# A planned 15-product kernel: one product of the first triple among the first plain products, two multiplications set aside, and loads in another order

## The chip, the core and the metric

The kernel runs on one core of one Trainium2 chip. The metric is the device time of one execution in microseconds (us). The core has a matrix engine (PE), a vector engine (DVE), a scalar engine (ACT), GpSimd (POOL) and a sync engine (SP) that only issues transfers and waits. Each engine works through its own instructions in order.

## The reference

```python
batch, m, k, n = 16, 512, 1024, 768
y1 = np.matmul(x, w1)          # x: (16, 512, 1024), w1, w2: (1024, 768)
y2 = np.matmul(x, w2)
return (np.tanh(y1) * y2).astype(np.float32)
```

All inputs and the output are 32-bit floats in HBM.

## The kernel before

**The work.** The 8192 rows of x are 64 row tiles of 128 rows. The columns of both weights are cut into three blocks of 512: `a` (w1's first 512 columns), `b` (w2's first 512) and `g` (the last 256 of w1 beside the last 256 of w2). K is cut into two halves of 512, four slices of 128 each. Everything is multiplied in 16-bit floats and summed in 32-bit PSUM banks, of which there are eight.

**Two ways of multiplying.** The first four row tiles (HEAD = 4) are done plainly: eight matmuls for each tile and block (`plain`, `mm`, L420), tanh on ACT, the multiplication by y2 on DVE. The `b` block of tile 3 is kept for the end. The other 60 row tiles are done three at a time, as 20 triples. For a triple a 3x2 by 2x3 block product would take 18 block products; a table `C_OPS` (L24) does it in 15, `p0` to `p14`, each of four matmuls (`product`, L442), on sums and differences of x blocks (`A_SUMS`, made on DVE by `x_sum`, L411) and of weight blocks (`B_SUMS`, `w_sum`, L402). Between the products ACT copies banks (`c_copy`, L447: names copy..., seed...) and DVE adds them (`c_add`, L450: add...); ACT then takes tanh (t, th) and DVE multiplies (m on 512 columns, mh on 256; `c_mul`, L460). Blocks are named by bits: x block 1, 2 are the two K halves of a triple's row 0, 4 and 8 those of row 1, 16 and 32 those of row 2; weight blocks 1, 2, 4 are a, b, g of the first K half, 8, 16, 32 those of the second. So p7 = x block 16 times weight block 1: the first half of row tile HEAD + 2 = 6 with the first four `a` slices. Its bank is copied by ACT (copy376) into the arena.

**How x and the weights arrive.** The first four x tiles come as half tiles of 32-bit floats on SP's queue (`load_first`, L337), DVE casts each half (`cast_x`), PE transposes it (`transpose_pe`, L368), and ACT or DVE moves the transposed half out of PSUM (`evacuate`, L374). The `a` slices come on ACT's and SP's queues, the `g` slices on SP's, into 14 slots of the `arena`, and are cast by DVE or ACT (`cast_w`). Behind a gate on POOL (L483), which waits for the first `g` cast, POOL's queue loads the eight `b` slices with a cast on the way, then the row tiles 6, 4, 5 whole, also with a cast (`load_x`, L352). Those three are transposed on PE; from row tile 7 on POOL loads and SP transposes by DMA (`transpose`, L377). The load of a later tile waits on POOL for a one-column copy from an earlier transposed tile (`hold_loads`, L480).

**What sets the order.** `Planner` (L75) lists every operation with costs, due times and dependencies, plays them once through, and writes the instructions in the order of the planned starts. The products' order is fixed by hand: `PE_ORDER` for one triple (a plus shifts a product into the next triple's time), `FIRST_ORDER` for the first triple, `LAST_ORDER` for the last; `plan.strict` keeps it. `START`, `lands`, `LANDING` and `hold` are assumed times by which the plan is made; on the chip semaphores decide.

```python
position["p" + entry.rstrip("+"), i] = (i + (entry[-1] == "+")) * 15 + n
...
rows_in = (HEAD + 2, HEAD, HEAD + 1)
...
in_order = on_sp[4:] + late + [f"x{mt}" for mt in rows_in]
```

Output tiles: four for the plain row tiles, nine that the triples take in turn (`out_tile`, L414). SP stores them.

Of the kernel before, what the change touches and what calls it, by code (L numbers as in the profile page):

```python
# [69 lines left out]
FIRST_ORDER = "7 10 1 6 12 9 11 14 8"  # L70
# [156 lines left out]
def kernel(  # L227
# [53 lines left out]
    S_NAMES = [o[3] for o in C_OPS if o[1] in ("copy", "add") and o[3][0] == "s"]  # L281
    arena = once.tile([P, len(S_NAMES) * C_BUFS * F], f32, name="arena")
# [3 lines left out]
    early_x = once.tile([P, len(A_SUMS) * S_BUFS * KH * P // 2], f32, name="early_x")  # L286
    x_first = [early_x[:, mt * K:(mt + 1) * K] for mt in range(HEAD)]
# [8 lines left out]
    def xh_place(mt):  # L296
        return (mt - HEAD) % XH_BUFS

    def xh_before(mt):
        return next((m for m in range(mt - 1, 1, -1) if xh_place(m) == xh_place(mt)), None)  # L300
# [35 lines left out]

    def load_first(e, mt, h):  # L337
        pin(nc.sync.dma_start(x_first[mt][:, half(h)], xf[mt][:, half(h)]))

    def cast_x(e, mt, h):  # L340
        copy(e, xh(mt)[:, half(h)], x_first[mt][:, half(h)])
# [10 lines left out]
    def load_x(e, mt):  # L352
        pin(nc.gpsimd.dma_start(xh(mt), xf[mt]))  # L353
# [87 lines left out]

    def product(e, i, dst, a, b, begins):  # L442
        for k in range(KH):
            pin(nc.tensor.matmul(place(i, dst), x_operand(i, a)[:, k, :], w_rhs(b, k),  # L444
                                 start=begins and k == 0, stop=k == KH - 1, skip_group_check=True))
# [17 lines left out]

    def flag_1(e):
# [18 lines left out]
    def gate(e, s, k):  # L483
        pin(nc.gpsimd.tensor_copy(held, w_cols(s, k)[:, :1]))
# [5 lines left out]
    START = 28.6  # L490
    ORIGIN = START - 6 * SLOT

# [10 lines left out]
    plan.strict = [f"{p}.{i}" for _, i, p in sequence]  # L503
# [7 lines left out]
    in_order = on_sp[4:] + late + [f"x{mt}" for mt in rows_in]  # L511
# [3 lines left out]
    for n in in_order:  # L515
        now += 1.25 if n in in_order[-3:] else size[n[0]]
# [4 lines left out]
    for n, what in enumerate(on_sp):  # L521
# [3 lines left out]
        else:  # L525
            s, k = what[0], int(what[1])
            j = slices.index((s, k))
            old = [slices[i - SLOTS] for i in range(j, j + 1 + (s == "g")) if i >= SLOTS]
            op(f"L{what}", {"sp": 0.05}, 0.1 * n - 100, [], load_w, s, k, int(what[2]) if s == "g" else None, issued=before,
               behind=[f"c{a}{b}" for a, b in old], lands=lands[what])  # L530
    op("gate", {"pool": 0.1}, 0.0, ["c%s%d" % GATE], gate, *GATE)
    for n, what in enumerate(late):
        op(f"c{what}", {"pool": 0.58}, 0.1 * n, [], load_w, "b", int(what[1]), issued=[f"c{late[n - 1]}" if n else "gate"], lands=lands[what])
    for n, mt in enumerate(rows_in):
        op(f"L{mt}", {"pool": 0.58}, 1 + 0.1 * n, [], load_x, mt, issued=[f"L{rows_in[n - 1]}" if n else f"c{late[-1]}"],
           behind=[f"cx{m}{h}" for m in range(2, HEAD) for h in range(2) if xh_place(m) == xh_place(mt)], lands=lands[f"x{mt}"])
# [7 lines left out]
    all_casts = [f"c{s}{k}" for s, k in slices if s != "b"]  # L544
# [19 lines left out]
    for mt in rows_in:  # L564
        for h in range(2):
            by_pe(mt, h, lands[f"x{mt}"] - 2, f"L{mt}")
# [17 lines left out]
    def reuse_out(mt):  # L584
        return [f"st{mt - O_BUFS}"] if mt >= HEAD + O_BUFS else []
# [283 lines left out]
```

## Time and profile before

| | |
|---|---|
| median of 3 runs | 297.97 us (297.73 to 298.39) |
| the profiled execution | 297.88 us, of which the profile's span is 296.3 |
| granted TensorE clock, mean | 0.997 |
| busiest groups of PE | L444, bank<-b,early_x: 640 matmuls, 148.3 us; L444, bank<-b,xT: 240, 58.3 us |
| DMA queue 1 (hardware): 44.84 MB; queue 0 (software) | 16.78 MB |
| x tiles on POOL's queue, issue to landing | 6.8 us median |
| transposes on SP's queue, issue to landing | 6.9 us median |

In a timeline row stand the start in us, the duration, the engine, the line and operation, output<-input, how many instructions were merged, and in brackets the idle time of that engine ahead of the row and what ended it. Matmuls of 512 columns are shown with 0.38 us each though they start closer together, so a merged row hides small gaps. In a row of busy time by stage, each engine has its busy time and, in brackets, its number of instructions; then follow the granted clock, the busy share of the DMA queues (over 1 where several hold an engine) and GB/s. L numbers are lines of the kernel before.

### The profile page before, as it was taken

Reading aid. Unit: us, or ns where it says so; the run is one execution under the profiler, and the core shown is the slowest. Engines: PE = TensorE matmul, PEld = TensorE weight load, DVE = VectorE, ACT = ScalarE, POOL = GpSimd, SP = SyncE. Lnnn points to the kernel's source line nnn. Section 1 sums busy time; section 2 is a strip of 40 time slices with the busy share of each in tenths; the row PEclk is TensorE's granted clock in tenths of the full one; section 3 lists DMA queues with packets and bytes.
Section 4 is the critical chain, followed back from the end, with each engine's and each line's share of the span. In section 5 each row is a group of like instructions: output and inputs, shape, how many; then the busy total and the mean of one; then the engine's idle time right before and its main releaser. Section 6 shows DMA issues by size and latency. Waiting matters only on the chain. (4 is left out here: it accounts for less than half of the span.)

```text
span 296.3 us, 4677 instructions
## 1 busy us (share of the span) xinstructions
PE 289.6 (98%) x1374; PEld 131.9 (45%) x1374; DVE 257.4 (87%) x552; ACT 226.3 (76%) x453; POOL 49.2 (17%) x129
## 2 busy tenths in 40 slices
PE   7999999999999999999999999999999999999994
PEld 3344444444444444444444444444444444444442
DVE  1679899989999998888989898898989989898785
ACT  3586899699978979797797988768686776868442
POOL 0063033020213021102110120031012110000000
PEclk9999999999999999999999999999999999999998
DMA  6999999999999999999999999999999999340334
GB/s 215 388 307 204 183 160 149 229 197 237 224 253 271 215 198 252 237 144 253 233 234 162 221 191 218 195 310 223 221 235 232 261 269 298 127 162 25 136 141 164
DMA packets 84715, 63.51 MB, mean 214 GB/s; under 512 B 62800, under 2 KB 66896, under 8 KB 84688
## 3 DMA queue, kind: packets, MB, share of 16 engines
q1 hardware_dynamic: 73888, 44.84, 62.9%
q0 software_dynamic: 9792, 16.78, 37.2%
q10 hardware_dynamic: 1008, 1.57, 1.5%
q8 instruction: 11, 0.18, 0.3%
q14 instruction: 16, 0.13, 0.2%
HBM read 39.85 MB, written 25.17 MB: 219 GB/s over the span
## 5 line engine op out<-in xcount | busy, mean ns | idle before, releaser
L444 PE MATMUL bank<-b,early_x 128*128 128x512 f16 x640 | 148.3, 379 | 0.1
L444 PEld LDWEIGHTS <-early_x 128*128 128x128 f16 x800 | 78.1, 98 | 95.0 <-issue 0.7
L454 DVE TENSOR_TENSOR bank<-bank,arena 128x512 f32<-128x512 f32 x100 | 69.6, 697 | 14.4 <-ACT arena L448 8.8
L448 ACT ACTIVATE arena<-bank 128x512 f32<-128x512 f32 x100 | 59.4, 596 | 28.7 <-PE bank L444 28.5
L462 DVE TENSOR_TENSOR o<-o,bank 128x256 f32<-128x256 f32 (+1 forms) x132 | 64.3, 512 | 6.1 <-ACT o L457 5.4
L381 ACT ACTIVATE junk<-xh 128x1024 f16<-128x1024 f16 x60 | 63.3, 1054 | 0.2
L444 PEld LDWEIGHTS <-xT 128*128 128x128 f16 x400 | 39.0, 98 | 46.6 <-issue 0.3
L444 PE MATMUL bank<-b,xT 128*128 128x512 f16 x240 | 58.3, 379 | 0.0
L457 ACT ACTIVATE o<-bank 128x256 f32<-128x256 f32 (+1 forms) x80 | 34.5, 436 | 16.0 <-DVE bank L454 11.7
L444 PE MATMUL bank<-wh,xT 128*128 128x512 f16 x160 | 41.1, 379 | 0.0
L444 PE MATMUL bank<-wh,early_x 128*128 128x512 f16 x160 | 40.9, 379 | 0.0
L481 POOL CAST held<-xT 128x1 f32<-128x1 f16 x54 | 12.3, 227 | 159.4 <-DMA xT<-xh 159.3
L353 POOL DMA_DIRECT2D xh<-in_x_dram x60 | 31.9, 532 | 17.2 <-issue 7.7
L412 DVE TENSOR_TENSOR early_x<-early_x,xT 128x512 f16<-128x512 f16 x80 | 33.2, 419 | 0.5
L448 ACT ACTIVATE bank<-bank 128x512 f32<-128x512 f32 x40 | 21.5, 574 | 7.3 <-DVE bank L454 6.2
L457 ACT ACTIVATE o<-arena 128x512 f32<-128x512 f32 x40 | 25.1, 628 | 1.2 <-DVE arena L454 1.2
L421 PE MATMUL bank<-wh,xT 128*128 128x512 f16 x72 | 18.5, 379 | 0.5 <-DVE wh L359 0.3
L412 DVE TENSOR_TENSOR early_x<-xT,xT 128x512 f16<-128x512 f16 x40 | 16.8, 419 | 0.0
L412 DVE TENSOR_TENSOR early_x<-xT,early_x 128x512 f16<-128x512 f16 x40 | 16.8, 419 | 0.0
L454 DVE TENSOR_TENSOR bank<-arena,bank 128x512 f32<-128x512 f32 x20 | 13.9, 695 | 2.4 <-ACT o L457 0.9
L454 DVE TENSOR_TENSOR arena<-bank,arena 128x512 f32<-128x512 f32 x20 | 13.7, 683 | 0.2
L454 DVE TENSOR_TENSOR arena<-arena,bank 128x512 f32<-128x512 f32 x20 | 13.6, 681 | 0.0
(47 smaller groups left out, 134.7 us busy)
## 6 DMA issues: line engine op xcount, KB each, us to landing
out_dram<-o SPq DMA_DIRECT2D x58, 384.0 KB, 5.3
xh<-in_x_dram POOLq DMA_DIRECT2D x60, 256.0 KB, 6.8
arena<-in_w_dram SPq DMA_DIRECT2D x12, 256.0 KB, 5.6
early_x<-in_x_dram SPq DMA_DIRECT2D x8, 256.0 KB, 5.0
arena<-in_w_dram ACTq DMA_DIRECT2D x4, 256.0 KB, 5.9
wh<-in_w_dram POOLq DMA_DIRECT2D x8, 128.0 KB, 5.1
out_dram<-o SPq DMA_DIRECT2D x4, 256.0 KB, 6.5
xT<-xh SPq DMA_TRANSPOSE x57, 6.9
```

Source lines behind the costliest of these rows:

```text
L353: pin(nc.gpsimd.dma_start(xh(mt), xf[mt]))
L381: pin(nc.scalar.activation(junk[:, :src.shape[-1]], src, ACT.Abs, scale=scale, accum_out=sums[:, column:column + 1]))
L412: pin(engine[e].tensor_tensor(x_operand(i, v), x_operand(i, a), x_operand(i, b), OP[how]))
L421: pin(nc.tensor.matmul(bank(chain)[:, :rhs.shape[-1]], xt(mt)[:, k, :], rhs, start=first, stop=k == KO - 1, skip_group_check=True))
L444: pin(nc.tensor.matmul(place(i, dst), x_operand(i, a)[:, k, :], w_rhs(b, k), start=begins and k == 0, stop=k == KH - 1, skip_group_check=T ...
L448: pin(nc.scalar.activation(place(i, dst), place(i, src), ACT.Copy, scale=float(sign)))
L454: pin(nc.vector.tensor_tensor(place(i, dst), a, b, ALU.add if signs == (1, 1) else ALU.subtract))
L457: pin(nc.scalar.activation(out_tile(HEAD + 3 * i + r)[:, lo:lo + n], place(i, src)[:, :n], ACT.Tanh, scale=float(sign)))
L462: pin(nc.vector.tensor_tensor(o, o, place(i, src)[:, at:at + n], ALU.mult))
L481: pin(nc.gpsimd.tensor_copy(held, xt(mt)[:, 0, :1]))
```

## The change

Six things change; the rest follows from them in the plan.

1. The first half of row tile 6 (`x60`) is loaded on SP as 32-bit floats, sixth in order, into a free arena slot (`STAGED`), cast by DVE (`cx60`), transposed by PE and evicted.
2. `p7` of the first triple leaves `FIRST_ORDER` and the strict order; it is due at 13.0, among the plain `a` products. What remains of the first triple is ordered 10 6 1 12 9 11 14 8.
3. POOL's queue carries, behind the gate, `b0 b4 b1 b5 x61 x4 b2 x51 x50 b6 b3 b7`: second half of tile 6, tile 4, the halves of tile 5, with the `b` slices between.
4. `m0` and `m2` of the first triple: ACT copies the bank into an output tile that is still free (those of row tiles 11 and 10), and DVE multiplies from there later.
5. In every triple the row tiles are loaded and transposed in the order 2, 0, 1 instead of 0, 1, 2.
6. A write to an arena slot waits for the casts out of that slot alone, not for all casts; the slots are dealt in another order. Row tile 0 is stored in one piece. The absolute sums of the second triple are due later.

```diff
-FIRST_ORDER = "7 10 1 6 12 9 11 14 8"
+FIRST_ORDER = "10 6 1 12 9 11 14 8"
...
-    LANDING = {HEAD + 6: 5.8, HEAD + 7: 4.1, HEAD + 8: 3.9}
+    LANDING = {HEAD + 6: 4.4, HEAD + 7: 4.1, HEAD + 8: 3.9}
+    rows = list(range(HEAD)) + [HEAD + 3 * i + r for i in range(TRIPLES) for r in (2, 0, 1)]
+    turn = {mt: n for n, mt in enumerate(rows)}
...
+    ASIDE = {"m0": (HEAD + 7, 55.0), "m2": (HEAD + 6, 54.0)}
...
+    S_NAMES.insert(1, S_NAMES.pop(0))
...
+    STAGED = SLOTS - 2
...
     def xh_place(mt):
-        return (mt - HEAD) % XH_BUFS
+        return (turn[mt] - HEAD) % XH_BUFS
...
+    def x_staged(mt, h):
+        return x_first[mt][:, half(h)] if mt < HEAD else arena[:, STAGED * F:(STAGED + 1) * F]
...
-    def load_x(e, mt):
-        pin(nc.gpsimd.dma_start(xh(mt), xf[mt]))
+    def load_x(e, mt, cols=slice(0, K)):
+        pin(nc.gpsimd.dma_start(xh(mt)[:, cols], xf[mt][:, cols]))
...
+    def slot_casts(name):
+        n = S_NAMES.index(name) * C_BUFS
+        return [f"c{s}{k}" for j, (s, k) in enumerate(slices) if s != "b" and n <= j % SLOTS < n + C_BUFS] + [f"cx{HEAD + 2}0"] * (n <= STAGED < n + C_BUFS)
...
+    def c_aside(e, r, src, borrowed):
+        pin(nc.scalar.copy(out_tile(borrowed)[:, :F], place(0, src)))
+
+    def aside_mul(e, r, borrowed):
+        o = out_tile(HEAD + r)[:, :F]
+        pin(nc.vector.tensor_tensor(o, o, out_tile(borrowed)[:, :F], ALU.mult))
...
+    P7 = 13.0
...
+    position["p7", 0] = 0
...
-    plan.strict = [f"{p}.{i}" for _, i, p in sequence]
+    plan.strict = [f"{p}.{i}" for _, i, p in sequence if (p, i) != ("p7", 0)]
+    slot_of[0, "p7"] = P7
...
-    on_sp = "x00 x10 x20 x30 x01 x11 a4 a5 x21 a6 x31 a7".split() + [f"g{k}{t}" for k in range(KH) for t in range(2)]
-    late = [f"b{k}" for s, k in slices if s == "b"]
-    rows_in = (HEAD + 2, HEAD, HEAD + 1)
-    GATE = ("g", 0)
+    on_sp = "x00 x10 x20 x30 x01 x60 x11 a4 a5 x21 a6 x31 a7".split() + [f"g{k}{t}" for k in range(KH) for t in range(2)]
+    by_pool = "b0 b4 b1 b5 x61 x4 b2 x51 x50 b6 b3 b7".split()
+    GATES = {"b0": ("cg0", w_cols("g", 0)[:, :1])}
...
+    op(f"cx{HEAD + 2}0", {"dve": 0.37}, lands["x60"] - 1, ["Lx60"], cast_x, HEAD + 2, 0,
+       behind=[f"cx{m}{h}" for m in range(2, HEAD) for h in range(2) if xh_place(m) == xh_place(HEAD + 2)])
...
-                    before = [f"{r}.{i - C_BUFS}" for r in readers[o[3]]] if i >= C_BUFS else all_casts
+                    before = [f"{r}.{i - C_BUFS}" for r in readers[o[3]]] if i >= C_BUFS else slot_casts(o[3])
...
+            elif i == 0 and name in ASIDE:
+                borrowed, at = ASIDE[name]
+                op(f"y{name}.0", {"act": 0.5}, due + 1, [n for n in needs if n[0] != "t"], c_aside, r, o[4], borrowed, chains=chains)
+                op(f"{name}.0", {"dve": 0.6}, at + 6, [f"y{name}.0"] + [n for n in needs if n[0] == "t"], aside_mul, r, borrowed, hold=at)
+                outs[mt].insert(0, f"{name}.0")
...
-            for t in range(2 if mt < 2 else 0):
+            for t in range(2 if mt == 1 else 0):
...
-    for mt in range(BY_PE, MT):
-        back = xh_before(mt)
+    for n, mt in list(enumerate(rows))[BY_PE:]:
+        back, last, held_by = xh_before(mt), rows[n - 1], rows[max(n - AHEAD, BY_PE)]
```

More of the change, by code (lines that the diff above doesn't have):

```diff
@@ L296, in xh_place @@
     def xh_place(mt):
-        return (mt - HEAD) % XH_BUFS
+        return (turn[mt] - HEAD) % XH_BUFS
     def xh_before(mt):
-        return next((m for m in range(mt - 1, 1, -1) if xh_place(m) == xh_place(mt)), None)
+        return next((m for m in rows[turn[mt] - 1:1:-1] if xh_place(m) == xh_place(mt)), None)
     pin = tc.keep_in_program_order
@@ L514 @@
     now = 9.2
-    for n in in_order:
-        now += 1.25 if n in in_order[-3:] else size[n[0]]
+    for n in arrivals:
+        now += 1.25 if n in by_pool and n[0] == "x" and len(n) == 2 else size[n[0]]
         lands[n] = now + (LAG if now > LAG_FROM else 0.0)
@@ L563 @@
         op(f"D{mt}", {"act": 1.05}, START + 8, [f"Lx{mt}0", f"Lx{mt}1"], abs_x, mt, hold=11 + 4 * mt)
-    for mt in rows_in:
+    for mt in rows[HEAD:BY_PE]:
         for h in range(2):
-            by_pe(mt, h, lands[f"x{mt}"] - 2, f"L{mt}")
+            by_pe(mt, h, x_loads[mt, h][1] - 2 - 0.1 * h * (mt == HEAD + 1), x_loads[mt, h][0])
     def made(mt):
```

61 lines of the change are left out of this document (38 added, 23 removed).

## The prediction

> **What bounds the kernel now.** I read the page's busy shares and the two rows of slices first, then busy time by stage, then the timeline of the first 45 us.
>
> ```profile
> span 296.3 us, 4677 instructions
> ...
> PE 289.6 (98%) x1374; PEld 131.9 (45%) x1374; DVE 257.4 (87%) x552; ACT 226.3 (76%) x453; POOL 49.2 (17%) x129
> ...
> PE   7999999999999999999999999999999999999994
> ...
> DMA  6999999999999999999999999999999999340334
> ```
>
> PE is busy in every slice but the first and the last, so the time is PE's work plus the holes in its queue. A busy share hides small holes, because a matmul's modelled 0.38 us overlaps the next one. So I count matmuls in stages:
>
> ```profile
> core 0: us, PE busy (x) PEld busy (x) DVE busy (x) ACT busy (x) POOL busy (x), PEclk, DMA share, GB/s
> ...
> 48.00:76.00 28.00, 28.00 (x132) 12.60 (x131) 26.55 (x63) 24.72 (x52) 6.82 (x18) 1.00 1.13 208
> 10.63:17.15 6.52, 6.13 (x39) 2.85 (x39) 3.43 (x9) 4.55 (x9) 0.00 (x0) 1.00 1.07 368
> 28.60:37.00 8.40, 8.27 (x56) 4.28 (x55) 7.53 (x18) 6.71 (x14) 0.48 (x2) 1.00 1.12 185
> 37.00:282.00 245.00, 245.00 (x1138) 111.02 (x1136) 222.72 (x476) 197.47 (x399) 40.09 (x107) 1.00 1.05 211
> ```
>
> From 37 to 282 us, 1138 matmuls take 245.00 us: 0.2153 us a slot, 0.861 us a product of four, and no hole. Nothing is to be won there; it can only be lost. The holes lie ahead of 37 us. The granted clock is 1.00 throughout. In the stage of the a products (10.63 to 17.15) the loads set the pace:
>
> ```profile
> 10.73 0.43 DVE L359 CAST xh<-early_x 128x512 f16<-128x512 f32 x1 [0.18 <-DMA early_x<-in_x_dram]
> ...
> 11.50 0.39 PE L371 MATMUL bank<-ident_h,xh 128*128 128x128 f16 x4
> ...
> 11.92 0.59 ACT L357 COPY xT<-bank 128x512 f16<-128x512 f16 x1 [0.28 <-PE bank L371]
> ...
> 12.37 1.03 PE L421 MATMUL bank<-wh,xT 128*128 128x512 f16 x4
> ...
> 13.04 0.43 DVE L359 CAST xh<-early_x 128x512 f16<-128x512 f32 x1 [0.53 <-DMA early_x<-in_x_dram]
> ...
> 13.52 0.40 PE L371 MATMUL bank<-ident_h,xh 128*128 128x128 f16 x4
> ...
> 13.71 0.43 DVE L359 CAST wh<-arena 128x512 f16<-128x512 f32 x1 [0.24 <-DMA arena<-in_w_dram]
> ...
> 14.19 1.02 PE L421 MATMUL bank<-wh,xT 128*128 128x512 f16 x4 [0.27 <-DVE wh L359]
> ...
> 15.05 0.39 PE L371 MATMUL bank<-ident_h,xh 128*128 128x128 f16 x4
> 15.10 0.43 DVE L359 CAST wh<-arena 128x512 f16<-128x512 f32 x1 [0.28 <-DMA arena<-in_w_dram]
> ...
> 15.27 1.11 PE L421 MATMUL bank<-wh,xT 128*128 128x512 f16 x4
> ...
> 16.67 0.43 DVE L359 CAST wh<-arena 128x512 f16<-128x512 f32 x1 [1.15 <-DMA arena<-in_w_dram]
> ...
> 17.15 1.24 PE L421 MATMUL bank<-wh,xT 128*128 128x512 f16 x5
> ```
>
> Each cast on DVE waits for a DMA, and PE for the cast. Four transposes take 0.22 us (15.05 to 15.27). The stage's 39 instructions are 16 transposes (0.88 us), one matmul begun before it, and 22 matmuls (4.74 us): 5.62 us of work in 6.52, so **0.90 us is lost**. The first g product starts at 17.15, 0.05 us behind the cast of 16.67: there too the load ends the wait.
>
> **The change, part by part.** *p7 and its half tile.* The load of row tile 6's first half becomes the sixth on SP, the place whose cast now starts at 10.73. All later loads on SP fall one place back; between 10.73 and 15.10 six places take 4.37 us, 0.73 each, and 13.04 to 13.71 is 0.67. I take **0.70 us** (bounds 0.67 and 0.73). The cast of g0 moves to 17.37 and the first g product to 17.85. Into that stage come p7's four matmuls (0.861) and the half tile's transposes (0.22), 1.08 us that leave the later queue. Since both ends are set by the same load, the gain is 1.08 - 0.70 = **0.38 us**; the loss left in the stage is 0.52.
>
> Does p7 arrive in time? As built, PE runs the transposes at 11.50, then four matmuls and another half tile's transposes, then p7 at 11.50 + 0.22 + 0.22 + 0.86 = 12.80. Its operand is cast by 11.16, evicted by ACT from 11.92 (0.42 behind the transposes, as in the row above) to 12.51: 0.29 us of cover. Behind that eviction ACT holds the next eviction, an absolute sum, p7's copy and another eviction; I cost that at nothing (bounds 0 to 0.3, the cover), because one of the later evictions is handed to DVE, which stood idle 1.15 us before 16.67. The staging slot in the arena is free at 11.16, five microseconds before the first g cast: nothing.
>
> *The loads on POOL.* The gate still hangs on g0's cast, so the stream starts 0.70 us later. In place of eight b slices and then three row tiles it carries b0 b4 b1 b5, half of tile 6, tile 4, b2, the two halves of tile 5, b6 b3 b7.
>
> ```profile
> L350 POOL DMA_DIRECT2D wh<-in_w_dram x8: 537/568/669, 17.5 to 21.3; - x8
> ...
> DMA to landing us min/median/max: 3.9/5.1/5.5
> ...
> L353 POOL DMA_DIRECT2D xh<-in_x_dram x2: 565/580/596, 21.9 to 22.4; - x2
> ...
> DMA to landing us min/median/max: 6.2/6.6/6.9
> ...
> L353 POOL DMA_DIRECT2D xh<-in_x_dram x1: 535/535/535, 24.0 to 24.0; - x1
> ...
> DMA to landing us min/median/max: 6.6/6.6/6.6
> ```
>
> The last b lands at 21.3 + 5.5 = 26.8, the row tiles at 28.1, 29.3 and 24.0 + 6.6 = 30.6: 1.25 us a tile, 0.63 a half or a b. Counting these as units, b7 was the 8th and is now the 13th: one unit before 30.6, and 0.70 later, 30.7. PE reaches its first use, by the built order, after 53 matmuls, 5 half-tile transposes and p10: 17.85 + 11.41 + 1.10 + 0.86 = 31.22. Cover **0.5 us**. Tile 4 ends unit 7: 26.2 + 0.7 = 26.9, used after 43 matmuls and one set of transposes at 27.33: cover **0.4 us**. So I cost the new order at nothing; without cover it costs what the landing slips beyond 0.4.
>
> Halving loads could cost something by itself. The 128 KB b slices land 0.77 us apart (21.4 to 26.8 in seven steps), the 256 KB tiles 1.25: a fixed part of at most 0.3 a load by these rows, 0.6 for the two loads that the stream has more, of which the cover takes 0.5. The Trainium skill puts it higher: "DMA: Bandwidth & Descriptors", section "Anatomy of one DMA — SWDGE (gpsimd) path", fits about 2.0 us fixed per DMA, and its section Bandwidth advises batching to 1 MiB; by that, as an estimate, the two loads would cost 4 us and the sum would be a loss. The steps of 0.77 us disagree with it as long as many loads are in flight.
>
> *The first triple.* Here the other hole lies:
>
> ```profile
> 32.15 1.29 DVE L412 TENSOR_TENSOR early_x<-early_x,xT 128x512 f16<-128x512 f16 x3
> 32.34 4.92 PE L444 MATMUL bank<-b,early_x 128*128 128x512 f16 x20
> ...
> 34.63 0.69 DVE L454 TENSOR_TENSOR bank<-bank,arena 128x512 f32<-128x512 f32 x1
> ```
>
> Twenty matmuls without a hole are 0.38 + 19 x 0.2153 = 4.47 us; the row says 4.92: **0.45 us lost**. p6, second of them, waits for the third of the three sums, which ends at 33.44, against 32.34 + 0.86 = 33.20; p9 waits for the addition that ends at 35.32. In the built order p6 comes behind b7's first use, at 31.44, and its last operand is transposed at 17.85 + 47 matmuls + four sets of transposes + p10 = 29.71, evicted by 30.72 and summed by 31.25 if DVE is free. DVE is 90% busy there, so I leave 0.15 us and take **0.30** (bounds 0 and 0.45). p9 now has p1, p12 and two plain matmuls between it and p6: its addition has two microseconds.
>
> *Two multiplications set aside.*
>
> ```profile
> L435 DVE TENSOR_TENSOR o<-o,y 128x512 f32<-128x512 f32 x3 | 2.1, 685 | 0.0
> L431 ACT COPY y<-bank 128x512 f32<-128x512 f32 x3 | 1.6, 624 | 0.0
> ...
> 42.30 0.74 DVE L462 TENSOR_TENSOR o<-o,bank 128x256 f32<-128x256 f32 x2
> ```
>
> DVE is spared two pairs of 0.74 us near 43 us and given two of 0.69 near 58; ACT gets two copies of 0.62. PE has no hole in either place, so this is worth nothing by itself (0 to 0.3 lost, if ACT's copies push back an eviction). The stores of tiles 4 and 6 go out later, and no one waits: nothing. The end of the program keeps its order but for eight narrow matmuls moved up among products: nothing, plus or minus 0.1.
>
> The sum on the profiled execution of 297.88: 297.88 - 0.38 - 0.30 = 297.20. The median shown, 297.97, is 0.09 above that execution, so **297.3**.
>
> **The rivals.** *The later loads take it back.* If the POOL stream slips by about 0.9 us more than I reckon, PE waits 0.5 at tile 4 or b7 and little is left: about 297.8. For it: the cover is only 0.4 to 0.5, and DMA share is over 1.0 in each stage above. Against: the bytes are the same, and the stream kept close to 0.63 us a unit through slices and tiles alike.
>
> *Rows in the order 2, 0, 1 (slower).* p7 wants row 2 first, but DVE's sums want rows 0 and 1, and these now come one transposition later. In the fifth triple:
>
> ```profile
> L378 SPq DMA_TRANSPOSE xT<-xh x1: 1471/1471/1471, 60.9 to 60.9; - x1
> ...
> DMA to landing us min/median/max: 7.5/7.5/7.5
> ...
> L378 SPq DMA_TRANSPOSE xT<-xh x1: 1982/1982/1982, 65.5 to 65.5; - x1
> ...
> DMA to landing us min/median/max: 8.5/8.5/8.5
> ...
> 73.64 0.42 DVE L412 TENSOR_TENSOR early_x<-early_x,xT 128x512 f16<-128x512 f16 x1
> ```
>
> The sum at 73.64 reads row 1, which landed at 68.4 and would land third, at 74.0. DVE, ahead by 0.7 us now, would stand about 1.0 us, with the additions for p13 and the evictions that free banks behind it. The third and the fourth triple stand about as close, and three such waits, 3 us, meet 28.00 - 26.55 = 1.45 us of DVE slack from 48 to 76, and some 1.6 us reach PE: 297.3 + 1.6 = **298.9**. It decides once the waits pass that slack. Against: the first PE product that needs such a sum comes microseconds later, and p7's own row comes earlier.
>
> *p7 is not early in effect.* If its eviction comes over 0.3 us late, PE, which runs in order, waits in front of it, and the 0.38 is gone: 297.6 to 297.7.
>
> *A fixed price per load.* If each load paid by itself what the first b paid from issue to landing, 3.9 us, the two more would put b7 7.8 us late, 7.3 beyond its cover: 304.6. The steps of 0.77 us speak against it. By the skill's 2.0 us it would be 300.8.
>
> **How the numbers follow.** Forecast 0.62 (by itself 297.0 to 297.7: the bounds of 0.38, of 0.30 and of the end, not all losses at once); loads take it back 0.15; row order 0.13; p7 late 0.08; fixed price 0.02. The range 296.8 to 298.3 holds the forecast, the first and the third rival, and the mildest outcomes of the second. About 0.2%, 0.60 us, is what can be told from no change. Below 297.37 lies some 0.45, most of the forecast's mass; beyond 298.57 the row order and the fixed price, 0.13 rounded down for the row order's milder outcomes; between, 0.42.
>
> **What would show it.** The g0 cast at 17.3 to 17.4 and the first g product at 17.8 to 17.9, with p7 among the a products and 0.5 us lost in that stage. PE without a hole from there to 31 us. The run of first products short of its 0.45 loss. Still 0.2153 us a slot from 37 us on. I am wrong if PE waits for a DMA between 24 and 32 us, if DVE's sums wait for a transposition between 48 and 76 and the slots there widen, or if the first g product comes later than 18.2.

## The result, and the profile after

The changed kernel takes 302.88 us in the median of 22 runs (297.89 to 321.91), the kernel before 297.86 us beside it (297.64 to 304.70, 22 runs). The ratio is 1.0063, 95% interval 1.0045 to 1.0081: **slower by 0.6%, about 1.9 us**, where 0.7 us less had been forecast. By the medians of all runs it is 5.0 us. The ratio leaves out every run more than 1.5% above the fastest of its kernel, 12 of the 22 after (the profiled execution of 305.15 us below among them) and one of the 22 before, so a hole in this profile counts only where a variant's profile of a run that stays shows the same. In the rows of a run, L numbers are lines of that run's own kernel: in the changed one L456 is a product, L420 a sum of x blocks, L469 tanh, L466 an addition, L474 a multiplication.

The page of the changed kernel: the span, PE's busy time, and the slices of PE and of the transfers.

```profile
span 303.6 us, 4689 instructions
...
PE 292.0 (96%) x1374; PEld 132.3 (44%) x1374; DVE 255.4 (84%) x552; ACT 224.5 (74%) x454; POOL 50.8 (17%) x130
...
PE   7999999999999999998979999999999999999992
...
DMA  6999999999999999999999999999999999941234
```

The same 1374 matmuls stand in 7.3 us more. Busy time by stage says where, first after, then before (columns as in the prediction):

```profile
10.63:17.58 6.95, 6.95 (x47) 3.69 (x46) 4.29 (x11) 6.08 (x12) 0.00 (x1) 1.00 1.07 371
28.60:37.00 8.40, 8.40 (x47) 3.94 (x45) 8.01 (x18) 5.04 (x11) 1.26 (x3) 1.00 1.05 188
...
62.00:92.00 30.00, 29.55 (x136) 12.99 (x135) 27.28 (x66) 25.50 (x56) 5.25 (x13) 1.00 1.18 206
92.00:136.00 44.00, 44.00 (x205) 19.97 (x204) 39.97 (x84) 36.66 (x77) 7.28 (x19) 1.00 1.19 190
136.00:160.00 24.00, 20.45 (x86) 8.66 (x85) 15.69 (x35) 15.19 (x32) 4.11 (x11) 0.93 1.13 212
```

```profile
62.00:92.00 30.00, 30.00 (x141) 13.62 (x140) 28.15 (x66) 26.89 (x58) 5.01 (x15) 1.00 1.16 220
92.00:136.00 44.00, 44.00 (x206) 19.92 (x205) 40.25 (x83) 36.77 (x75) 8.90 (x24) 1.00 1.17 224
136.00:160.00 24.00, 24.00 (x113) 10.92 (x112) 21.42 (x46) 20.36 (x42) 3.59 (x11) 1.00 1.22 228
```

From 62 to 92 us PE starts 136 matmuls instead of 141: 5 x 0.2153 = 1.1 us lost. From 136 to 160 it loses 27 more, 5.8 us, which belongs to this execution. The rest is at the two ends. The start, by the timeline of the changed kernel, then one row of the kernel before:

```profile
10.70 0.43 DVE L367 CAST xh<-arena 128x512 f16<-128x512 f32 x1 [0.25 <-DMA arena<-in_x_dram]
...
12.83 1.03 PE L456 MATMUL bank<-wh,xT 128*128 128x512 f16 x4
...
17.08 0.43 DVE L367 CAST wh<-arena 128x512 f16<-128x512 f32 x1 [0.74 <-DMA arena<-in_w_dram]
17.58 1.24 PE L429 MATMUL bank<-wh,xT 128*128 128x512 f16 x5
...
37.82 1.03 PE L456 MATMUL bank<-wh,xT 128*128 128x512 f16 x4
```

```profile
38.85 1.03 PE L444 MATMUL bank<-wh,xT 128*128 128x512 f16 x4
```

p7 of the first triple runs at 12.83, the first g cast at 17.08, and p7 of the second triple at 37.82 instead of 38.85: **the start gains 1.03 us**, more than forecast. Then the transpositions. SP's transposes of the third and of the fifth triple, after; below, the third triple's before:

```profile
L386 SPq DMA_TRANSPOSE xT<-xh x3: 1270/1950/2817, 40.6 to 45.4; - x3
...
DMA to landing us min/median/max: 4.2/6.3/7.4
...
L386 SPq DMA_TRANSPOSE xT<-xh x3: 1232/1302/2558, 58.1 to 66.1; - x3
...
DMA to landing us min/median/max: 3.3/8.7/10.4
```

```profile
L378 SPq DMA_TRANSPOSE xT<-xh x3: 1344/2178/2521, 41.0 to 45.7; - x3
...
DMA to landing us min/median/max: 4.1/5.9/7.1
```

The last of the third triple lands at 45.4 + 4.2 = 49.6, and before at 45.7 + 4.1 = 49.8. **PE comes 1.0 us earlier, the rows come 0.2 us earlier.** In the fifth triple the third transposition lands at 66.1 + 8.7 = 74.8. What waits for it, what stands around it, and what happens later in this execution:

```profile
58.78 1.29 DVE L481 TENSOR_TENSOR o<-o,o 128x512 f32<-128x512 f32 x2
...
71.95 0.63 ACT L469 ACTIVATE o<-arena 128x512 f32<-128x512 f32 x1 [0.88 <-DMA out_dram<-o]
...
73.12 1.02 PE L456 MATMUL bank<-wh,early_x 128*128 128x512 f16 x4 [0.25 <-ACT bank L460]
...
74.91 0.43 DVE L420 TENSOR_TENSOR early_x<-early_x,xT 128x512 f16<-128x512 f16 x1 [1.51 <-DMA xT<-xh]
...
77.76 0.59 PE L456 MATMUL bank<-wh,xT 128*128 128x512 f16 x2 [0.16 <-ACT o L469]
...
138.11 1.15 ACT L469 ACTIVATE o<-arena 128x512 f32<-128x512 f32 x2 [2.57 <-DMA out_dram<-o]
...
153.08 0.63 ACT L469 ACTIVATE o<-arena 128x512 f32<-128x512 f32 x1 [4.08 <-DMA out_dram<-o]
...
154.25 1.08 PE L456 MATMUL bank<-b,early_x 128*128 128x512 f16 x4 [2.11 <-ACT arena L460]
```

DVE's sum of row 1 waits 1.51 us, and ACT's tanh waits four times for the store of an output tile: 0.88 us at 71.95, 2.57 at 138.11, 4.08 at 153.08, just ahead of PE's longest stop, and 1.0 at 168. From 40 to 92 us PE's loss is four holes: 0.16 us at 41.4, 0.20 at 64.1, 0.41 at 73.1 (behind the store), 0.33 at 77.8 (behind the late row). No wait for a transfer stands ahead of the one at 64.1: DVE had been busy without a break of 0.1 us since 54.6, the 1.29 us of the two set-aside multiplications included. In the kernel before, DVE has time to spare at that place:

```profile
61.47 0.70 DVE L454 TENSOR_TENSOR bank<-bank,arena 128x512 f32<-128x512 f32 x1 [0.26 <-PE bank L444]
62.78 0.75 DVE L462 TENSOR_TENSOR o<-o,bank 128x256 f32<-128x256 f32 x2 [0.61 <-ACT o L457]
```

Last, the end. The changed kernel's transfers from 298 us on and its last stores, then the same of the kernel before:

```profile
GB/s 307 73 22 22 29 51 307 395 410 322 359 329 329 461 329 322 329 322 293 139 7 7 15 7 22 22 22 22 29 15 0 0 0 0 0 0 0 0 0 0
...
q8 instruction: 1, 0.02, 1.0%
...
L426 SPq DMA_DIRECT2D out_dram<-o x2: 332/332/332, 298.3 to 299.0; - x2
...
DMA to landing us min/median/max: 2.3/3.7/3.7
```

```profile
q8 instruction: 1, 0.02, 1.2%
...
L418 SPq DMA_DIRECT2D out_dram<-o x2: 332/332/333, 292.4 to 293.1; - x2
...
DMA to landing us min/median/max: 2.0/2.1/2.2
```

The last stores take 3.7 us instead of 2.2. Each slice of the GB/s row is 0.14 us: the bulk moves at some 330 GB/s until 300.7, and then 10 slices, 1.4 us, at 7 to 29, about a sixteenth, as of one of sixteen engines that is behind. Queue q8 (its kind is "instruction") carries program code, 16 KB a time, 11 times in either kernel. Its last fetch starts at 299.9 us in the changed kernel, among these stores; in the kernel before at 288.6 (the second q8 row is of 285 to 289.4 us), ahead of them. From the issue of the last store to the end of the span it is 303.6 - 298.96 = 4.6 us, before 296.3 - 293.10 = 3.2: **1.4 us lost at the very end**.

### The profile page after: what moved, and what is told of

Read it like the earlier page. It is cut to its first block, busy times and chain, and to the rows that moved or that the text cites. A ratio compares the mean times of both kernels' runs of the same rounds, so it can differ in the third digit from the quotient of the medians.

```text
span 303.6 us, 4689 instructions
## 1 busy us (share of the span) xinstructions
PE 292.0 (96%) x1374; PEld 132.3 (44%) x1374; DVE 255.4 (84%) x552; ACT 224.5 (74%) x454; POOL 50.8 (17%) x130
## 5 line engine op out<-in xcount | busy, mean ns | idle before, releaser
L456 PE MATMUL bank<-b,early_x 128*128 128x512 f16 x640 | 148.5, 379 | 2.1 <-ACT arena L460 2.1
L456 PEld LDWEIGHTS <-early_x 128*128 128x128 f16 x800 | 78.3, 98 | 99.0 <-issue 5.4
L466 DVE TENSOR_TENSOR bank<-bank,arena 128x512 f32<-128x512 f32 x100 | 69.6, 696 | 19.2 <-ACT arena L460 16.3
L474 DVE TENSOR_TENSOR o<-o,bank 128x256 f32<-128x256 f32 (+1 forms) x128 | 61.9, 516 | 9.2 <-ACT o L469 7.1
L460 ACT ACTIVATE arena<-bank 128x512 f32<-128x512 f32 x100 | 57.8, 597 | 15.4 <-PE bank L456 15.3
L456 PEld LDWEIGHTS <-xT 128*128 128x128 f16 x400 | 39.1, 98 | 48.7 <-issue 3.8
L456 PE MATMUL bank<-b,xT 128*128 128x512 f16 x240 | 59.1, 383 | 0.0
L469 ACT ACTIVATE o<-bank 128x256 f32<-128x256 f32 (+1 forms) x80 | 34.8, 440 | 24.1 <-DVE bank L466 22.2
L456 PE MATMUL bank<-wh,early_x 128*128 128x512 f16 x160 | 41.8, 385 | 1.7 <-ACT bank L460 1.7
L456 PE MATMUL bank<-wh,xT 128*128 128x512 f16 x160 | 41.0, 379 | 0.2 <-ACT o L469 0.2
L500 POOL CAST held<-xT 128x1 f32<-128x1 f16 x54 | 13.4, 247 | 162.5 <-DMA xT<-xh 162.4
L469 ACT ACTIVATE o<-arena 128x512 f32<-128x512 f32 x40 | 25.1, 631 | 16.9 <-DMA out_dram<-o 8.5
L361 POOL DMA_DIRECT2D xh<-in_x_dram x61 | 32.7, 537 | 19.4 <-issue 5.5
L420 DVE TENSOR_TENSOR early_x<-early_x,xT 128x512 f16<-128x512 f16 x80 | 33.6, 421 | 2.0 <-DMA xT<-xh 1.5
L429 PE MATMUL bank<-wh,xT 128*128 128x512 f16 x72 | 19.5, 379 | 0.3 <-ACT xT L365 0.2
L420 DVE TENSOR_TENSOR early_x<-xT,xT 128x512 f16<-128x512 f16 x40 | 16.8, 420 | 0.0
L420 DVE TENSOR_TENSOR early_x<-xT,early_x 128x512 f16<-128x512 f16 x40 | 16.8, 419 | 0.0
L466 DVE TENSOR_TENSOR arena<-bank,arena 128x512 f32<-128x512 f32 x20 | 13.7, 685 | 1.9 <-ACT arena L460 1.9
L466 DVE TENSOR_TENSOR bank<-arena,bank 128x512 f32<-128x512 f32 x20 | 13.8, 691 | 0.1
L389 ACT ACTIVATE junk<-wh 128x768 f16<-128x768 f16 x16 | 13.6, 852 | 0.1
```

Source lines behind the costliest of these rows:

```text
L361: pin(nc.gpsimd.dma_start(xh(mt)[:, cols], xf[mt][:, cols]))
L389: pin(nc.scalar.activation(junk[:, :src.shape[-1]], src, ACT.Abs, scale=scale, accum_out=sums[:, column:column + 1]))
L420: pin(engine[e].tensor_tensor(x_operand(i, v), x_operand(i, a), x_operand(i, b), OP[how]))
L429: pin(nc.tensor.matmul(bank(chain)[:, :rhs.shape[-1]], xt(mt)[:, k, :], rhs, start=first, stop=k == KO - 1, skip_group_check=True))
L460: pin(nc.scalar.activation(place(i, dst), place(i, src), ACT.Copy, scale=float(sign)))
L466: pin(nc.vector.tensor_tensor(place(i, dst), a, b, ALU.add if signs == (1, 1) else ALU.subtract))
```

## The experiments

All times are medians in us. "End" is the time from the last store's issue to the end of the span, "hole" the longest time beyond 0.216 us between the starts of two matmuls from 40 to 100 us, both of the profiled execution.

| run | median (range), runs | ratio to before (95%) | end | hole |
|---|---|---|---|---|
| before | 297.8 to 297.9 in each set | 1 | 3.2 | under 0.1 |
| after | 302.88 (297.89 to 321.91), 22 | 1.0063 (1.0045 to 1.0081) | 4.6 | 0.41 |
| e1_rows_012 | 299.06 (297.36 to 305.13), 12 | 1.0026 (0.9992 to 1.0060) | 3.2 | 1.39 |
| e2_rows_201_alone | 299.47 (297.96 to 310.67), 12 | 1.0029 (1.0006 to 1.0052) | 3.2 | 0.94 |
| e3_not_aside | 300.42 (297.74 to 303.62), 9 | 1.0082 (1.0047 to 1.0117) | 3.6 | 0.31 |
| e4_start_alone | 299.52 (298.38 to 303.65), 12 | 1.0048 (1.0027 to 1.0070) | 4.7 | 0.27 |
| e5_narrow_fill | 305.63 (301.10 to 312.81), 8 | 1.0168 (1.0142 to 1.0194) | 3.2 | 1.70 |
| e6_short_stores | 299.30 (298.83 to 299.80), 6 | 1.0050 (1.0037 to 1.0063) | 4.7 | 0.48 |
| e7_both | 300.10 (299.67 to 300.76), 6 | 1.0071 (1.0059 to 1.0084) | 3.2 | 1.02 |
| e8_before_short | 297.78 (297.60 to 298.09), 11 | 0.9994 (0.9982 to 1.0006) | 3.2 | 0.11 |
| e9_short_fill4 | 299.45 (297.52 to 299.95), 12 | 1.0045 (1.0029 to 1.0060) | 3.3 | 1.44 |
| e10_before_fill2 | 299.34 (297.80 to 299.89), 9 | 1.0039 (1.0023 to 1.0055) | 4.6 | 0.27 |
| e11_fill4 | 303.34 (299.83 to 306.23), 6 | 1.0114 (1.0066 to 1.0162) | 3.2 | 1.18 |
| e12_fill4_ahead5 | 305.42 (298.76 to 318.35), 10 | 1.0024 (0.9969 to 1.0078) | 4.0 | 1.22 |
| e13_sums_late | 301.64 (298.68 to 309.11), 6 | 1.0096 (1.0061 to 1.0132) | 3.3 | 2.06 |
| e14_sums_late_not_aside | 301.36 (299.97 to 301.82), 5 | 1.0107 (1.0090 to 1.0124) | 3.3 | 1.53 |
| e15_before_fill4 | 298.03 (297.69 to 300.79), 12 | 1.0016 (1.0000 to 1.0032) | 3.2 | 0.30 |
| e16_sums_late_short | 299.21 (297.54 to 301.35), 8 | 1.0040 (1.0014 to 1.0066) | 3.3 | 0.80 |
| e17_rows_mixed_not_aside | 298.15 (297.20 to 304.82), 12 | 0.9997 (0.9966 to 1.0029) | 3.2 | 1.56 |
| e18_rows_mixed | 298.20 (297.23 to 314.77), 13 | 1.0009 (0.9975 to 1.0042) | 3.2 | 0.24 |

### The parts of the change, one by one

e1 is the changed kernel with the old row order, e2 the kernel before with the new one (and its bookkeeping), e3 the changed kernel with nothing set aside, e4 both of e1 and e3:

```diff
# e1 and e4
-    rows = list(range(HEAD)) + [HEAD + 3 * i + r for i in range(TRIPLES) for r in (2, 0, 1)]
+    rows = list(range(MT))
# e3 and e4
-    ASIDE = {"m0": (HEAD + 7, 55.0), "m2": (HEAD + 6, 54.0)}
+    ASIDE = {}
```

> The changed kernel with one part undone: row tiles are again loaded and transposed in the order 0, 1, 2 within a triple. Row-order theory (the sum that reads row 1 of the fifth triple stands 1.5 us for the third transposition, PE loses 0.9 us between 63 and 78 us, and the transfers fall behind from there): the first 41 us stay 1.1 us ahead of the kernel before and nothing is lost after, 296.6 to 297.0 in every run, spread under 1 us. Set-aside theory (the stores of tiles 4 and 6 come late and crowd the transfers): as the changed kernel, 298 to 310, widely spread. Transfer-limit theory (transfers set the pace from 60 us on, so whatever starts earlier waits later): 297.8 or more, no better than the kernel before.

> The kernel before with one part of the change alone: rows in the order 2, 0, 1. Row-order theory: slower than before by 1 to 5 us and widely spread, with a DVE wait for a transposition between 72 and 75 us. Set-aside theory: 297.9, as before. Transfer-limit theory: 297.9 to 298.5, since nothing starts earlier.

> The changed kernel with m0 and m2 of the first triple multiplied at once from their banks, as before; all else as changed. Row-order theory: as the changed kernel, 298 to 310, widely spread. Set-aside theory: 296.6 to 297.0, spread under 1 us. Transfer-limit theory: 297.8 or more.

> The early p7 and the new order of the first loads without the row order 2, 0, 1 and without the set-aside multiplications. Row-order theory: 296.6 to 297.2, since the set-aside ones cost and bring next to nothing. Set-aside theory: 296.6 to 297.0 too. Transfer-limit theory: 297.8 or more.

By the median none goes back to 297.8, and none gains; e1's interval still holds 1. The end is late in e4 alone: in e1 and e3 the last fetch starts at 291.0 and 291.4 us. e2 did what the row-order theory said of it, slower by the median (1.6 us, 0.9 by the ratio), widely spread, with DVE waiting for a transposition from 73.5 us on; the transfer theory's 297.9 to 298.5 us missed there. But e1, with the old order, came nowhere near that theory's 296.6 to 297.0. So the row order costs something, and neither it nor the setting aside is the whole cause. One timeline row each of e4 (PE), e1 (DVE) and e2 (DVE):

```profile
38.68 1.04 PE L456 MATMUL bank<-wh,xT 128*128 128x512 f16 x4 [0.55 <-DMA xT<-xh]
```

```profile
50.04 0.43 DVE L420 TENSOR_TENSOR early_x<-xT 128x512 f16<-128x512 f16 x1 [2.61 <-DMA xT<-xh]
```

```profile
75.48 0.43 DVE L414 TENSOR_TENSOR early_x<-early_x,xT 128x512 f16<-128x512 f16 x1 [1.95 <-DMA xT<-xh]
```

With rows 0, 1, 2 and the new start, e4's PE stands in front of p7 of the second triple for row 2, transposed third, and e1's DVE stands 2.61 us for row 0 of the third triple itself, transposed first. With 2, 0, 1 and the old start, e2's DVE waits 1.95 us in the fifth triple for row 1, transposed third. **With the new start, someone stands in front of a row in whatever order; with the old start, from 38 us on, only in the new order.** That leaves the transfers to be tried next.

### Fewer bytes, and the code moved

e6 cuts the stores of row tiles 4 to 15 (seven eighths of these rows are left unwritten), e8 does that to the kernel before, e5 splits the fillers (matmuls on a constant ahead of 9 us), e7 is e5 with e6:

```diff
# e6, e7, e8
-        pin(engine[e].dma_start(of[mt][:, lo:lo + n], out_tile(mt)[:, lo:lo + n]))
+        rows_out = 16 if HEAD <= mt < HEAD + 12 else P
+        pin(engine[e].dma_start(of[mt][:rows_out, lo:lo + n], out_tile(mt)[:rows_out, lo:lo + n]))
# e5, e7
-    FILL = 512, 512, 256
+    FILL = (64,) * 20
```

> The changed kernel with its two fillers in 20 matmuls of 64 columns each instead of 512, 512 and 256: the same columns, 34 matmuls and 34 weight loads more in TensorE's code, all of them before 9 us. Code-fetch theory: TensorE's code comes in fetches of 16 KB, of which the last is at 288.6 us in the kernel before, ahead of the last stores, and at 299.9 us in the changed one, among them, where the last three stores take 3.7 us instead of 2.2 us. With 68 instructions more ahead of it the fetch comes some 7 us earlier: the last stores land in 2.0 to 2.6 us again and the time falls by about 1.4 us, to 297.5 us in the undisturbed runs. Transfer theory (the transpositions between 36 and 80 us land no earlier than before, so the head start is lost there): the tail has no part in it, the last stores may do as they like, and the time stays at 299 us or more with a wide spread.

> The changed kernel with the stores of rows 4 to 15 cut to 16 of 128 partitions (seven eighths of these twelve rows are left unwritten), in the same order of work. Transfer theory: with 4.1 MB less to move between 45 and 100 us the transpositions land 1 us or more earlier from the third triple on, the waits of DVE's sums for the third transposition (1.51 us at 74.9 us) and of tanh for stores (2.57 us at 138 us) are gone, TensorE's product 1000 of 1200 starts at 245.8 us instead of 246.9 us of the kernel before, and the spread of the runs narrows to less than 1 us; the time is 296.7 us, or 298.2 us with the late code fetch. Code-fetch theory alone: holes in the middle are chance, the time is that of the changed kernel, 299 to 303 us.

> Both edits at once in the changed kernel: narrow fillers and the stores of rows 4 to 15 cut to 16 of 128 partitions. If the transfers and the late code fetch are the two causes: 296.6 to 297.0 us in nearly all runs, 1 us under the kernel before, as the start promises (the second triple's p7 at 37.8 us against 38.9 us). If only the transfers are: as the run with short stores alone. If only the code fetch is: as the run with narrow fillers alone.

> The kernel before with the stores of rows 4 to 15 cut to 16 of 128 partitions. Transfer theory: its products have no hole from 35 us on, so there is nothing to give back, 297.8 us within 0.2 us. If short stores make any kernel faster (through the tail, or through the clock), this falls too, by the same as the changed kernel, and the run with short stores says nothing of the head start.

With the stores cut, the changed kernel's spread falls from 24 us to 1.0, and the kernel before stays where it was: **the wide spread comes from the transfers.** (e9 and e16 below also cut the stores, and spread by 2.4 and 3.8 us.) Busy time from 62 to 92 us, of e6, then of e8:

```profile
62.00:92.00 30.00, 29.68 (x139) 13.30 (x137) 28.19 (x67) 26.09 (x57) 8.29 (x22) 1.00 1.15 192
```

```profile
62.00:92.00 30.00, 30.00 (x141) 13.58 (x140) 28.13 (x66) 26.89 (x58) 7.45 (x20) 1.00 1.17 183
```

Even so it isn't faster. e6's span is 1.3 us over e8's (297.7 and 296.4). Its end is 4.7 us and e8's 3.2, which is 1.4 of it; the start's gain, 0.8 us over the kernel before in this run, is given back in the middle (holes of 0.48 us at 63.8 and smaller ones). These holes aren't all made by late rows: after 40 us DVE waits once in e6 for a transposition, 0.18 us at 61.45, and the hole of 0.48 stands behind tanh on ACT:

```profile
64.54 1.02 PE L457 MATMUL bank<-wh,xT 128*128 128x512 f16 x4 [0.32 <-ACT o L470]
```

All 11 profiles with the two multiplications set aside have a hole of 0.16 to 1.44 us between 64 and 68 us. Of the nine without them only e14 has one there, of 1.34 us, with DVE waiting 1.29 us for a transposition. I had expected 298.2 us with the late end; 299.30 is 1.1 us over it, the middle's share.

e5 and e7 answer for the code. The last fetch now starts 10 us ahead of the last matmul, and the end is 3.2 us. But the first one moves too, from 21.0 to 15.5 us, into the weight loads: holes of 1.04 us (e5) and 1.56 us (e7) at 17.5 us. More than the end's gain goes there, which I hadn't expected.

### Four instructions more or fewer

e9 (on e6) and e11 (on the changed kernel) have four TensorE instructions more, e15 the kernel before with four more, e10 with four fewer; e12 is e11 with loads further ahead.

```diff
# e9, e11, e12, e15
-    FILL = 512, 512, 256
+    FILL = 512, 512, 128, 128
# e10
-    FILL = 512, 512, 256
+    FILL = 512, 512
# e12
-    AHEAD, FREE = 4, 3
+    AHEAD, FREE = 5, 4
```

> The changed kernel with the stores of rows 4 to 15 cut to 16 of 128 partitions, as before (299.3 us, 298.8 to 299.8; last three stores 3.7 us each, with TensorE's last 16 KB of code fetched at 294.0 us, 2.2 us after the last matmul), and the last 256 columns of each filler in two matmuls of 128: four instructions more on TensorE in all, at no cost at the start. Code-fetch theory: the last fetch moves ahead of the last stores, to between 287 and 291 us, these land in 2.2 us, and the time falls by 1.4 us to 297.9 us. If the late stores have nothing to do with the fetch, or if four instructions don't move it: 299.3 us.

> The kernel before without the last 256 columns of each filler: four instructions fewer on TensorE, all before 8 us, and nothing else. Code-fetch theory: the last fetch, at 288.6 us in the kernel before and 3.3 us ahead of its last matmul, moves behind it, among the last stores, these take 3.7 us and the time rises by 1.4 us to 299.3 us, as in the changed kernel, which has one instruction fewer on TensorE than before. If the fetch is no cause, or four instructions don't move it: 297.8 us.

> The changed kernel, all stores whole, with the last 256 columns of each filler in two matmuls of 128 (four instructions more on TensorE). Both causes together: the tail is short again, 297.4 to 297.6 us in the best runs, but the waits for transpositions and stores in the middle stay, and with them a spread of several us; median 299 to 301 us. If the late fetch were the whole loss: 297.4 us in nearly all runs.

> The changed kernel with the four instructions and with x rows loaded five transpositions ahead of use instead of four (four free of the hold at the start instead of three); the order of work on the engines is planned anew by that. Transfer theory, where the hold on the loads is what keeps the transpositions late: they land 1 us or more earlier from the third triple on, the spread narrows, 297 to 298 us. Where the DMA engines themselves are the limit (busy share 9 of 10 and more in every slice from 20 to 255 us): more in flight lands no earlier, each transposition takes longer, 299 us or more.

> The kernel before with the last 256 columns of each filler in two matmuls: four TensorE instructions more, the opposite of the run with four fewer (299.3 us). Code-fetch theory: the last fetch stays ahead of the last stores, at 288 us or before, and the time stays at 297.8 us. If any shift of the code costs, it rises as it did with four fewer.

e10 is the plainest run of the study: the kernel before, nothing changed but two matmuls of 256 columns on a constant, left out before 8 us. Its transfers from 292 us on, and its last stores:

```profile
q8 instruction: 1, 0.02, 0.9%
...
L418 SPq DMA_DIRECT2D out_dram<-o x2: 332/332/333, 292.7 to 293.4; - x2
...
DMA to landing us min/median/max: 2.4/3.7/3.7
```

The fetch moved from 288.6 to 294.3 us, the stores take 3.7 us, and six of nine runs lie at 299.3 to 299.9. **The late code fetch costs 1.4 us, in a kernel that has nothing of the change.** e15, with four more, stays at 298.0. e9, e11 and e12 have an end of 3.3, 3.2 and 4.0 us, so four more do mend the end of the changed kernel, but e9 then has a hole of 1.44 us at 63.7 us, and e11 and e12 pay at the start. The first fetch starts at 20.5 us instead of 21.0, and a weight load comes late, by ACT's row of e11:

```profile
22.91 1.14 ACT L365 CAST wh<-arena 128x512 f16<-128x512 f32 x2 [1.65 <-DMA arena<-in_w_dram]
```

In the changed kernel all such waits of ACT sum to 0.4 us. e12, e13, e14 and e16 have the wait too (1.5 to 1.8 us), e9 with its fetch at 20.8 us has none. That the fetch makes the load late is likely, and not shown. Loading further ahead (e12) brought nothing that can be seen.

### The sums held longer

e13 holds two sums of triples 2 to 6 longer, with e11's filler; e14 also sets nothing aside; e16 is e13 with the stores cut.

```diff
-               hold=needed(i, v) - S_AHEAD if i > 1 else 0.0,
+               hold=needed(i, v) - S_AHEAD + (1.5 if v in (3, 11) and i < 7 else 0.0) if i > 1 else 0.0,
```

> The changed kernel, all stores whole, with the last 256 columns of each filler in two matmuls (four TensorE instructions more) and with the sums S3 and S11 of triples 2 to 6 held 1.5 us longer in the plan. Theory of the sum's wait: DVE waits at most 0.3 us for a transposition between 48 and 95 us (1.5 us in the changed kernel), PE has no hole over 0.3 us there, product 200 of 1200 starts at 73.6 us or earlier (75.2 us in the run with four instructions alone), the runs lie between 297 and 299 us. Theory of late transpositions as such: the wait moves to PE's own p6 or p7, the hole is as long, 299 to 306 us.

> As the run with the sums held longer, and with nothing set aside in the first triple, so that rows 4 to 6 are stored from 49 us on instead of 61 us. Theory of the sum's wait: stores bunched at 61 us are gone as well, so this is the best version, 296.9 to 297.6 us in most runs, below the kernel before. Theory of late transpositions as such: 299 to 301 us, as without the longer hold.

> The sums held longer, four TensorE instructions more, and the stores of rows 4 to 15 cut to 16 of 128 partitions. Both theories take the holes away here if the sums' wait is what is left of them (1.44 us at 63.7 us in the run with cut stores and four instructions, 299.45 us): 297.0 to 297.3 us with a spread under 0.8 us, that is the start's gain kept. If the hole at 63.7 us has nothing to do with the sums: 299.4 us again.

All three missed what the theory of the sum's wait forecast and came within 0.4 us of what stood against it. DVE's sum in e13, and the matmul behind it:

```profile
78.83 0.42 DVE L420 TENSOR_TENSOR early_x<-early_x,xT 128x512 f16<-128x512 f16 x1 [2.10 <-DMA xT<-xh]
...
80.67 1.02 PE L456 MATMUL bank<-wh,xT 128*128 128x512 f16 x4 [1.90 <-DVE o L474]
```

The sum starts 3.9 us later on the clock than in the changed kernel, and has waited longer. The row is late, and asking for it later didn't help. That theory fell, and "late as such" stands, though the wait stayed with DVE and didn't move to PE's own p6 or p7. With the stores cut as well (e16) 0.80 us of hole is left.

### Another row order and the code put right

e17 and e18 take the rows as 2, 0, 1 in the first three triples and as 0, 1, 2 from the fourth on, and have their four TensorE instructions more at 28 us, behind the first fetch; e17 also sets nothing aside.

```diff
-    rows = ... for i in range(TRIPLES) for r in (2, 0, 1)]
+    rows = ... for i in range(TRIPLES) for r in ((2, 0, 1) if i < 3 else (0, 1, 2))]
...
+        cut = [0, n // 2, n] if chain == ("b", 2) and k in (3, 7) else [0, n]
+        for lo, hi in zip(cut, cut[1:]):
+            pin(nc.tensor.matmul(bank(chain)[:, lo:hi], xt(mt)[:, k, :], rhs[:, lo:hi], ...))
```

> The changed kernel with the rows in the order 2, 0, 1 in the first three triples and 0, 1, 2 from the fourth on, nothing set aside, and two matmuls of 512 columns near 28 us split in halves of 256 (four TensorE instructions more, behind the first code fetch). If the two causes are the late code fetch and the row that is asked for while it is still being transposed: the first fetch stays at 21.0 us with no hole at 22.7 us, the last is ahead of the last stores (tail 5.4 us instead of 6.8 us after the last product's start), no wait over 0.5 us between 36 and 90 us, 296.9 to 297.4 us in most runs, which would be faster than the kernel before. If the head start itself is what the transpositions can't feed, in whatever order: a hole of 0.5 us or more stands at a p7 of the third to fifth triple, and the time is 298 us or more.

> The same with the two multiplications set aside as in the changed kernel, so that the stores of rows 4 to 6 go out in a bunch at 61 us instead of from 49 us on. If the bunch costs (transpositions of the fourth and fifth triple landing over 8 us after their issue): 0.5 us or more over the run that sets nothing aside, with more spread. If setting aside is worth nothing either way: the same time within 0.3 us.

The end is short again in both (3.2 us), the first fetch stays at 20.9 and 21.2 us without a hole at 22.7, and the best runs come to 297.20 and 297.23 us, the forecast's 297.3. But the medians are 298.15 and 298.20: in e17's profile DVE still waits for transpositions three times, 3.6 us in all, and PE has holes of 1.56 us at 89.9, behind the longest of these waits (2.26 us), and of 0.55 us at 50.5, with 0.12 us of such a wait ahead of it. Against the changed kernel's ratio of 1.0063 this is 0.6% better, and no better than before. Setting aside or not is the same within 0.1 us.

## Why the prediction was wrong

- **The a-product stage: right, and too small.** The load of x60 pushes the g0 cast from 16.67 to 17.08 and the first g product from 17.15 to 17.58, 0.41 to 0.43 us instead of my 0.70. With 1.08 us of work moved in the stage gains 0.65, not 0.38. p7 at 12.83 stands where I put it (12.80).
- **The first triple: right.** The whole start gains 1.03 us; less 0.65, that leaves 0.38 here against my 0.30.
- **POOL's order at nothing: right.** PE is busy 8.40 of 8.40 us from 28.6 to 37, and has no hole of 0.1 us from 17.58 on. So "a fixed price per load" didn't show either, and p7 wasn't late. (POOL's queue has one load more than before, not two; the other is on SP.)
- **"Two multiplications set aside ... worth nothing": right in the times** as far as it can be told (e3 against after, e17 against e18), but not in the traces. They fill DVE's idle time near 62 us, and PE has a hole at 64 to 68 us in every profile that has them: 0.16 to 0.20 us in the six where it is smallest, within the "0 to 0.3 lost" of the prediction, which gave ACT's copies as the reason.
- **The step that failed first: "The end of the program keeps its order ...: nothing, plus or minus 0.1".** It is +1.4 us, by no operation of the end: the last code fetch meets the last stores. e10 makes this loss alone, and moving the fetch takes it away (e9 against e6). If the other runs of the changed kernel have it, as e6's and e4's profiles do and e1's and e3's do not, it is three quarters of the 1.9 us. What in the change moves the fetch isn't shown: e1's trace has as many TensorE instructions as the changed kernel's (2776, before 2777), and its fetch starts 2.1 us ahead of the last matmul, where the changed kernel's starts 2.1 us behind it.
- **The step that failed second: that the gain of the start is kept, since PE holds "0.2153 us a slot from 37 us on".** I compared landings with uses as the trace of before had them, and moved the landings for the new row order but not the uses, which come 1.0 us earlier. The transpositions of the third triple land only 0.1 to 0.2 us earlier, and the start's gain is spent between 41 and 78 us (1.1 us in the profiled execution; with the stores cut it goes too). Late rows are the larger part of what the variants show (holes of 0.71 us in e4, 1.39 in e1, 0.94 in e2, 1.56 in e17, 2.06 in e13), and not all of it: DVE's queue has no time left either. Holes of 0.31 us at 51 in e3, and of 0.27 and 0.30 us at 52 in e10 and e15, which have the old start, stand without any wait for a transfer between 45 us and the hole.
- **The rival "rows in the order 2, 0, 1"** had the wait: the fifth triple's sum stands 1.51 us at 74.91 for a row that landed at 74.8, where I had written 1.0 us and 74.0. Its price was off: one such wait in the changed kernel, not three, and e2, which has the order alone, loses 0.9 us of the 1.6. And the order isn't all: with 0, 1, 2 and the new start the wait goes to p7 (e4) or to the sum of the first row (e1).
- **"Later loads take it back"** named the transfers, at the wrong place: not the stream before 32 us, but the transpositions and the stores after 37.

What is shown: that a late fetch costs 1.4 us at the end, in both directions; that the spread comes with the transfers (e6 against after, e8 against before). What is only argued: that the head start itself uses up the slack of the transposed rows and of DVE; the landings and waits above agree, but each run has its hole elsewhere, and no run takes work off DVE alone. Open: why four instructions move the fetch by 5.7 us (e10) or not at all (e15, 288.8 us), why three of e10's nine runs are spared, and what delays a single transposition from 3 to 15 us.

## What to carry to other kernels

An earlier start is worth only as much as the feed behind it can follow: before counting a gain, set every later landing against its use moved up by that gain, each row in turn, and the idle time of the next busiest engine against it too. Where the end of a kernel is a chain of stores, look at the code queues in the list of transfers: a fetch of 16 KB among the last stores cost twice what this whole change was to gain, and a few instructions fewer moved it there. And a kernel whose runs agree within 0.3% (all but one of 22 here) can lose just that by a change that shortens its start.

## What the runs showed of the hardware that I had not expected

- **Program code shares the transfer engines.** TensorE's code comes in fetches of 16 KB, one in some 27 us; 186 of the 220 in these profiles take 0.9 to 1.2 us, the longest 4.1 us (e1). Beside such a fetch the last stores took 3.7 us instead of 2.2 (e10). The Trainium skill, "Runtime: NRT & Kernel Launch", section "Instruction fetch mechanics", has the 16 KB blocks and the sequential prefetch, and says the cost of crossing a block is mostly hidden; the blocks agree with the 11 fetches of q8 here, the cost does not where the fetch meets a transfer that someone waits for.
- **Half clock after a short stop.** Busy time by stage of the changed kernel, around the stop that ends at 154.25:

```profile
154.20:155.10 0.90, 0.85 (x4) 0.38 (x4) 0.87 (x2) 0.62 (x2) 0.00 (x0) 0.99 1.01 298
155.10:158.50 3.40, 3.40 (x9) 1.21 (x8) 2.85 (x8) 3.39 (x7) 0.71 (x2) 0.50 1.15 161
```

  PE stood 2.27 us, ran on at full clock for 0.9 us, and then had a granted clock of 0.50 for 3.4 us, another 1.7 us lost. Holes of up to 2.06 us (e13) were not followed by it; those of 2.27, 2.77 (e5) and 3.27 us (e18) were, and in one of 4.65 us (e5) the clock fell before PE went on. The Trainium skill, "TensorE: Matmul & The Clock Gate", section "What's actually happening", puts the drop behind an idle window of some 3.4 us that runs freely; here a stop of two thirds of that was enough.
- **A transposition by DMA took from 3.1 to 15.3 us to land** in the profiled execution of the changed kernel, with the same bytes each time.
